# A substitution with its operands turned round, its place in the order of a scan's steps, and the order of the projections beside it

## The chip, the cores and the metric

The kernel runs on one core of a Trainium2 chip. The metric is the time of one execution on the device, in microseconds (us). Five engines work beside each other, each through its own queue in a fixed order: TensorE (PE, matrix products, with its weight loads as PEld), VectorE (DVE), ScalarE (ACT), GpSimd (POOL) and SyncE (SP, which issues most of the DMAs). An engine that comes to an instruction whose input isn't there waits, and all behind it in its queue waits too.

## The reference

Two layers. In each, a normalised and modulated input `h` (768 tokens: 256 of context, 512 latent) is multiplied by one large matrix `w_in`; its columns feed three mixers, their gates and the merge:

```python
h = rms_norm(x, norm_g) * (1.0 + scale) + shift
za, ga, zb, gb, zc, gc, zg = jnp.split(h @ w_in, list(IN_CUTS), axis=-1)
ya = rwkv7_branch(za, ...)            # two scans over time, forward and backward
yb = dense_block_attention(...)       # from zb
yc = window_attention(...)            # from zc
m = sum(sigmoid(zg_n) * ((y_n * silu(g_n)) @ w_branch_out[n]))
x_new = x + gate * (m @ w_out)
```

The scan of the first mixer is the step `S <- S diag(w) - (S kk)(kk*a)^T + v k^T`, `y = S r`, for each of eight heads and two directions. The first layer gives an output for context and latent tokens, the second for the latent ones alone.

## The kernel before, in words

The scan is done in 12 chunks of 64 tokens (`NCH`), the eight heads and two directions beside each other. Within a chunk the recurrence is a triangular system, so each chunk needs the inverse of a triangular 64x64 matrix. `rwkv_inverse` (L654) makes them for four chunks at a time (`NS` = 4), in three groups (`NG`): for each 64x64 matrix it inverts the two 32x32 blocks on the diagonal by substitution on DVE and makes the third block from them with small matmuls (`zp`, L691, and `yp`, L699).

The substitution (L673 to L678) runs over `j` from 30 down to 1. For each `j` there are two DVE instructions over `j * (31 - j)` elements of each of 128 partitions: a product of a broadcast column and a broadcast row into `tmp` (L676), and its addition to `YK` (L678). `YK` is a view of `YB`, whose rows of 64 elements lie behind each other, so that in the view `Y3` (`p i j`) the last index steps over 64 elements, 256 bytes. Ahead of it stands a transposition on DVE (L666), behind it two more (L681, L682). The function is a generator. Its first part, up to the `yield` at `j` = 22, holds the loads of `TT` and the first nine pairs, the second goes to `j` = 12, the third to the transpositions; three more hold the small matmuls.

`rwkv` (L510) runs the scan. First comes group 0's inverse, then `FILL[l][1]` steps of other work to cover it, and then the twelve steps of the scan, `rwkv_step` (L705). Each step is cut in three: `Rp` from the state, `Up` with the inverse, `Sp` and `Yp` to the new state and the output; in between stand copies on ACT and DVE (L714, L727, L728) and the state's update on DVE (L738, L739). Between them stand parts of `scores` for the chunk after next (matmul `scps`, then L642 and L644 on DVE), of `readout` (L564) and of the fill. After each of the first three steps of a group one part of the next group's inverse is emitted (L557), in the fourth step the parts with matmuls (L552).

The fill is the rest of `h @ w_in`: `tiles` (L1454) is a generator over tiles of 128 columns, and `pace(n)` (L1468) takes `n` steps of it. A tile over both segments is 48 matmuls in 8 steps (the narrow tile `T_KR` has 5). Beside them, twice in a tile, `side` gives a piece of the modulation `ada` (matmul `modps`, then L261 and L269 or L272 on DVE). `proj` (L764) ends a tile: a "raw" tile is one copy on ACT for each segment; a "silu" tile is an ACT instruction (L777) and a DVE instruction (L779) for each, and only behind it is the PSUM bank free for the next tile. The tiles `g` have two banks (`GB`); a tile over both segments takes both. Each half tile needs a weight block that ACT splits (L165) and POOL subtracts (L166). The tiles of the last gate (`T_ZG`, "tanh") come last, and what the scan leaves of them stands between the matmuls of the later stages and then by itself (`gates`, L1496).

The order of the work: the scheduler puts each instruction into its engine's queue at build time, by a priority and by when it expects its inputs. `band(b)` sets the priority: `SERVE` comes first, then `B + 1` (the scan), `B + 3` (attention), `B + 4` (fill). Within a band the order of the program counts. `in_line()` (L148) keeps all TensorE instructions of the scan in the order of the program; the other engines' instructions are free to change places. The small matmuls `zp` of a group thus hold up everything behind them on TensorE until the substitution is done.

Of the kernel before, what the change touches and what calls it, by code (L numbers as in the profile page):

```python
# [14 lines left out]
ALU = mybir.AluOpType  # L15
# [4 lines left out]
P = 128  # L20
# [9 lines left out]
GB, RB, CB = 2, 3, 2  # L30


FILL = ((48, 36, 2, (2, 2, 2), (3, 3, 3), 2), (72, 56, 4, (2, 2, 2), (3, 3, 3), 2))

QUEUES = (("scalar", "sync", "sync", "scalar"), ("sync", "scalar", "sync", "sync"))

# [1 line left out]
NS, NG = 4, 3  # L38
# [22 lines left out]
def build(tc, A, out):  # L61
# [13 lines left out]
    @contextmanager  # L75
    def band(b):

        keep, mine = tc.cur_priority, bands.get(b, b * 1000000)
        tc.cur_priority = mine
        yield  # L80
        bands[b] = tc.cur_priority
        tc.cur_priority = keep
# [427 lines left out]
    def rwkv(l, D, last, DL, B, pace, zlast):  # L510

        with tc.tile_pool(name="rw", bufs=1, reuse_waits="tile") as rp:
            yo = rp.tile([P, 4, T], F32, name="yo")
            st = {"seen": set(), "S": None}
            parts, YB = {}, {}

            def scores(i):
                if i < NCH:
                    parts[i] = yield from rwkv_scores(l, last, rp, i)

            def invert(g):
                if g < NG:
                    YB[g] = rp.tile([P, 32, 64], F32, tag="YB", name="YB", bufs=2)
                    yield from rwkv_inverse(l, rp, g, YB[g])

            def rest(*gens):
                for g in gens:
                    for _ in g:
                        pass

            with band(B + 1):
                rest(scores(0), scores(1))
                ahead = invert(0)
                for _ in range(3):
                    next(ahead)
            with band(B + 4), tc.issue_after(zlast):
                pace(FILL[l][1])
            with band(B + 1), in_line():
                for _ in ahead:
                    pace(FILL[l][2])  # L540
                ahead = out = iter(())
                for i in range(NCH):
                    if i % NS == 0:
                        rest(ahead)
                        ahead = invert(i // NS + 1)
                    nxt = scores(i + 2)
                    step = rwkv_step(l, last, i, yo, st, DL, rp, parts.pop(i), YB[i // NS])
                    for n in FILL[l][3 if i % NS < NS - 1 else 4]:
                        next(step, None)
                        next(nxt, None)  # L550
                        if i % NS == NS - 1:
                            next(ahead, None)  # L552
                        next(out, None)
                        pace(n)
                    rest(step, nxt)
                    if i % NS < NS - 1:
                        next(ahead, None)  # L557
                    if i in READY and (i > 3 or not last):
                        rest(out)
                        out = readout(l, D, rp, yo, READY[i])  # L560
                for _ in out:
                    pace(FILL[l][5])

# [90 lines left out]
    def rwkv_inverse(l, rp, g, YB):  # L654
# [3 lines left out]
        for b0 in (0, 64):  # L658

            DMA.dma_start(TT[b0:b0 + 32], tt_d[l][b0:b0 + 32, :, cs])  # L660
            DMA.dma_start(TT[b0 + 32:b0 + 64, :, :, 0:32], tt_d[l][b0 + 32:b0 + 64, :, cs, 32:64])
        inv = rp.tile([P, 1536], F32, tag="inv", name="inv")
        MB, tmp = inv[:, 0:1024], inv[:, 1024:1536]
        YK = YB[:, :, 32:64]
        TT4 = TT.rearrange("p c s t -> p (c s) t")
        V.transpose(MB, TT4[:, :, 0:32].rearrange("p n j -> p j n"))  # L666

        M3 = MB.rearrange("p (j i) -> p i j", i=32)
        Y3 = YK.rearrange("p j i -> p i j")
        G.affine_select(YK, MB.rearrange("p (j i) -> p j i", i=32),  # L670
                        [[1, 32], [-1, 32]], ALU.is_gt, 0.0, base=0, channel_multiplier=0)
        V.memset(YB.rearrange("p n c -> p (n c)")[:, 32:2048:65], 1.0)
        for j in range(30, 0, -1):  # L673
            n = 31 - j
            t3 = tmp[:, 256 * (j % 2):256 * (j % 2) + j * n].rearrange("p (i c) -> p i c", c=n)
            V.tensor_tensor(t3, M3[:, 0:j, j:j + 1].to_broadcast([P, j, n]),  # L676
                            Y3[:, j:j + 1, j + 1:32].to_broadcast([P, j, n]), ALU.mult)
            V.tensor_tensor(Y3[:, 0:j, j + 1:32], Y3[:, 0:j, j + 1:32], t3, ALU.add)  # L678
            if j in (22, 12):
                yield  # L680
        V.transpose(YB[:, :, 0:32].rearrange("p n j -> p j n"), YK)  # L681
# [753 lines left out]
    for l in range(2):  # L1435
# [18 lines left out]
        def tiles():  # L1454

            zb = [(T_CQ + j, zb_d[l][j], (LAT,) if last and j < 2 else BOTH, "raw") for j in range(4)]
            zc = [(T_ZC + j, zb_d[l][4 + j], (LAT,) if last and j < 4 else BOTH, "raw") for j in range(6)]
            ga, gb, gc = ([(t + j, g_d[l][4 * n + j], segs, "silu") for j in range(4)]
                          for n, t in enumerate((T_GA, T_GB, T_GC)))
            todo = zb[2:] + zc[4:] + zc[:4] + zb[:2] + ga + gb if last else zb + ga + gb + zc  # L1460
            todo += gc + [(T_ZG + j, th_zg[l][j], segs, "tanh") for j in range(24)]
            for a in todo:
                yield from proj(l, hh, hl, *a, side)
                yield
# [193 lines left out]
```

## Time and profile before

| | |
|---|---|
| median of 3 runs | 2422.4 us (2420.09 to 2424.84) |
| the profiled execution's own time | 2427.43 us |
| its span in the trace | 2425.7 us |
| mean granted TensorE clock | 0.948 of full speed |
| TensorE busy | 2148.9 us (89%) |
| VectorE busy | 1271.8 us (52%) |
| substitution, L676 and L678, 360 instructions | 183.7 us of VectorE |

The profile is one execution. The busy share of an engine is a mean over stages, so what bounds a stage is read from that stage: how long TensorE was busy in it, and what ended its waits. The granted clock is given as a share of 2.4 GHz; the other level is 1.2 GHz. The first layer's scan, with its first inverse, lies at 360 to 640 us from the span's start, the second layer's at 1660 to 1940 us.

### The profile page before, as it was taken

The numbers are of one execution on the slowest core, as the hardware profiler recorded it, in microseconds if no ns is written. First come the engines' busy times: TensorE is split into PE (matmuls) and PEld (weight loads), VectorE is DVE, ScalarE is ACT, GpSimd is POOL, SyncE is SP. The second block draws the span as 40 slices with busy tenths as digits, with TensorE's granted clock in tenths as the row PEclk, the third lists the DMA queues.
The fourth block names the chain that finished last, engine by engine and source line by source line (L and its number), as shares of the span: only waits on it lengthen the run. The fifth ranks groups of instructions, "written<-read, shape, count | busy, mean of one in ns | idle before, by whom it ended". The sixth has DMA issues, their size and how long they took to land. (4 is left out here: it accounts for less than half of the span.)

```text
span 2425.7 us, 42832 instructions
## 1 busy us (share of the span) xinstructions
PE 2148.9 (89%) x16824; PEld 1647.0 (68%) x16824; DVE 1271.8 (52%) x2300; ACT 891.7 (37%) x1654; POOL 870.0 (36%) x699
## 2 busy tenths in 40 slices
PE   7986896887998999899888998799868998999989
PEld 4765674766887667766767786567656876666667
DVE  4475326865338664366135256725668457554423
ACT  3443211233354333543213345332323455434322
POOL 1255211111123344444334224553211144454564
PEclk9988998998999999999989999899978999999999
DMA  7155665555251012511686414566444262102385
GB/s 249 60 144 175 194 197 138 138 132 136 74 170 50 31 44 84 189 33 51 205 256 188 134 57 123 163 206 169 121 113 101 86 209 92 48 18 70 106 261 168
DMA packets 330442, 314.25 MB, mean 130 GB/s; under 512 B 112768, under 2 KB 239488, under 8 KB 330240
## 3 DMA queue, kind: packets, MB, share of 16 engines
q1 hardware_dynamic: 312432, 281.87, 39.5%
q10 hardware_dynamic: 17808, 29.63, 3.9%
q8 instruction: 133, 2.18, 0.4%
q14 instruction: 69, 0.57, 0.1%
HBM read 213.64 MB, written 97.78 MB: 128 GB/s over the span
## 5 line engine op out<-in xcount | busy, mean ns | idle before, releaser
L166 POOL TENSOR_TENSOR wl<-wf,wh 128x512 fp32r<-128x512 f32 x316 | 425.7, 1349 | 1064.0 <-ACT wh L165 977.2
L154 PE MATMUL g<-hh,wh 128*128 128x512 f32 (+1 forms) x1264 | 471.3, 373 | 19.2 <-DVE st L779 10.2
L154 PE MATMUL g<-hh,wl 128*128 128x512 f32 (+1 forms) x1264 | 457.0, 362 | 1.5 <-POOL wl L166 1.4
L154 PE MATMUL g<-hl,wh 128*128 128x512 f32 (+1 forms) x1264 | 456.4, 361 | 0.0
L165 ACT CAST wh<-wf 128x512 fp32r<-128x512 f32 x316 | 195.1, 619 | 500.7 <-PE g L154 249.3
L154 PEld LDWEIGHTS g<-hh,wh 128*128 128x128 f32 x1264 | 249.1, 197 | 71.9 <-issue 15.4
L154 PEld LDWEIGHTS g<-hh,wl 128*128 128x128 f32 x1264 | 249.3, 197 | 41.1 <-issue 7.9
L154 PEld LDWEIGHTS g<-hl,wh 128*128 128x128 f32 x1264 | 249.9, 198 | 40.1 <-issue 11.4
L886 POOL TENSOR_TENSOR acc<-acc,pe 128x512 f32<-128x512 f32 (+2 forms) x128 | 146.2, 1142 | 141.2 <-ACT pe L882 131.7
L882 ACT ACTIVATE pe<-stp 128x256 f32<-128x256 f32 (+2 forms) x224 | 114.4, 522 | 201.1 <-PE stp L154 194.4
L864 DVE TENSOR_REDUCE mx<-mps 128x1 f32<-128x384 f32 (+2 forms) x256 | 127.8, 535 | 69.2 <-PE mps L154 67.0
L154 PE MATMUL yps<-pe,vh 128*64 128x256 f32 (+1 forms) x704 | 133.3, 389 | 0.0
L678 DVE TENSOR_TENSOR YB<-YB,inv 128x30 f32<-128x30 f32 (+9 forms) x180 | 96.4, 536 | 5.3
L154 PE MATMUL g<-yh,wh 128*128 128x512 f32 (+1 forms) x224 | 81.4, 368 | 19.9 <-DVE zt L1368 11.4
L1368 DVE SCALAR_TENSOR_TENSOR zt<-zt,g 128x512 f32<-128x512 f32 (+1 forms) x56 | 31.7, 576 | 117.6 <-PE g L154 85.3
L676 DVE TENSOR_TENSOR inv<-inv,YB 128x30 f32<-128x30 f32 (+9 forms) x180 | 87.3, 485 | 8.5 <-issue 2.3
L777 ACT ACTIVATE st<-g 128x256 f32<-128x256 f32 (+1 forms) x108 | 56.6, 524 | 89.1 <-PE g L154 83.7
L154 PE MATMUL g<-yl,wh 128*128 128x512 f32 (+1 forms) x224 | 83.5, 374 | 6.1 <-POOL yl L1353 6.1
L154 PE MATMUL gc<-hh,wh 128*128 128x512 f32 x192 | 76.7, 400 | 8.6 <-ACT hh L325 4.5
L154 PE MATMUL g<-yh,wl 128*128 128x512 f32 (+1 forms) x224 | 80.4, 363 | 0.0
L154 PE MATMUL scps<-AR,BK 64*128 64x128 f32 (+1 forms) x768 | 65.5, 296 | 14.5 <-DVE TR L644 10.6
L154 PE MATMUL gc<-hl,wh 128*128 128x512 f32 x192 | 78.0, 406 | 0.1
(395 smaller groups left out, 4358.2 us busy)
## 6 DMA issues: line engine op xcount, KB each, us to landing
wf<-w_in SPq DMA_DIRECT2D x163, 256.0 KB, 3.1
wf<-ada_w SPq DMA_DIRECT2D x84, 256.0 KB, 4.0
wf<-w_in ACTq DMA_DIRECT2D x77, 256.0 KB, 3.0
bkd<-bk SPq DMA_DIRECT2D x16, 768.0 KB, 6.3
zt<-thzg SPq DMA_DIRECT2D x48, 256.0 KB, 3.8
wf<-w_bo SPq DMA_DIRECT2D x40, 256.0 KB, 3.5
thzg<-st SPq DMA_DIRECT2D x24, 384.0 KB, 2.4
md<-zt SPq DMA_DIRECT2D x32, 256.0 KB, 3.5
```

The costliest lines, as they stand in the source:

```text
L154: queued(TE.matmul(o, l, r, start=start, stop=stop, **kw))
L165: S.copy(wh, w32)
L166: eng.tensor_tensor(wl, w32, wh.bitcast(F32), ALU.subtract)
L676: V.tensor_tensor(t3, M3[:, 0:j, j:j + 1].to_broadcast([P, j, n]), Y3[:, j:j + 1, j + 1:32].to_broadcast([P, j, n]), ALU.mult)
L678: V.tensor_tensor(Y3[:, 0:j, j + 1:32], Y3[:, 0:j, j + 1:32], t3, ALU.add)
L777: S.activation(t[:, sl], p, AF.Tanh, scale=0.5)
L864: V.tensor_reduce(mx, ps, AX.X, ALU.max)
L882: S.activation(e, st, AF.Exp, scale=scale)
L886: G.tensor_tensor(acc, keep.pop(0, acc), e, ALU.add)
L1368: V.scalar_tensor_tensor(th, th, 1.0, p_, ALU.add, ALU.mult)
```

## The change

Four edits, in three functions and one table.

- The substitution holds the same numbers in the same places, but its two instructions run with the index of neighbouring elements innermost: `YK` itself is the operand instead of its turned view, and `M3` is viewed as `p j i`.
- The first part of `rwkv_inverse`, up to a new `yield`, now holds the loads of `TT` alone.
- In the scan, the next group's loads are emitted at the head of the group's first step, and right behind them all three parts of its substitution, in the band `B + 2`, which was not used before and comes after `B + 1`. Nothing is emitted after the first three steps any more.
- In the first layer `FILL[0][1]` is 48 instead of 36, and its projections run in the order `zb`, `zc`, `ga`, `gb` (raw ones first) instead of `zb`, `ga`, `gb`, `zc`. The second layer's table and order are as they were.

```diff
-FILL = ((48, 36, 2, (2, 2, 2), (3, 3, 3), 2), (72, 56, 4, (2, 2, 2), (3, 3, 3), 2))
+FILL = ((48, 48, 2, (2, 2, 2), (3, 3, 3), 2), (72, 56, 4, (2, 2, 2), (3, 3, 3), 2))
...
                 ahead = invert(0)
-                for _ in range(3):
+                for _ in range(4):
                     next(ahead)
...
                     if i % NS == 0:
                         rest(ahead)
+
                         ahead = invert(i // NS + 1)
+                        next(ahead, None)
+                        with band(B + 2):
+                            for _ in range(3):
+                                next(ahead, None)
...
                     rest(step, nxt)
-                    if i % NS < NS - 1:
-                        next(ahead, None)
...
             DMA.dma_start(TT[b0 + 32:b0 + 64, :, :, 0:32], tt_d[l][b0 + 32:b0 + 64, :, cs, 32:64])
+        yield
...
-        M3 = MB.rearrange("p (j i) -> p i j", i=32)
-        Y3 = YK.rearrange("p j i -> p i j")
+        M3 = MB.rearrange("p (j i) -> p j i", i=32)
...
-            t3 = tmp[:, 256 * (j % 2):256 * (j % 2) + j * n].rearrange("p (i c) -> p i c", c=n)
-            V.tensor_tensor(t3, M3[:, 0:j, j:j + 1].to_broadcast([P, j, n]),
-                            Y3[:, j:j + 1, j + 1:32].to_broadcast([P, j, n]), ALU.mult)
-            V.tensor_tensor(Y3[:, 0:j, j + 1:32], Y3[:, 0:j, j + 1:32], t3, ALU.add)
+            t3 = tmp[:, 256 * (j % 2):256 * (j % 2) + j * n].rearrange("p (c i) -> p c i", c=n)
+            V.tensor_tensor(t3, M3[:, j:j + 1, 0:j].to_broadcast([P, n, j]),
+                            YK[:, j + 1:32, j:j + 1].to_broadcast([P, n, j]), ALU.mult)
+            V.tensor_tensor(YK[:, j + 1:32, 0:j], YK[:, j + 1:32, 0:j], t3, ALU.add)
...
-            todo = zb[2:] + zc[4:] + zc[:4] + zb[:2] + ga + gb if last else zb + ga + gb + zc
+            todo = (zb[2:] + zc[4:] + zc[:4] + zb[:2] if last else zb + zc) + ga + gb
```

## Rows read from the trace of the kernel before

**Rows 1.** The page's part 1: busy time, share of the span, instructions of each engine.

```profile
PE 2148.9 (89%) x16824; PEld 1647.0 (68%) x16824; DVE 1271.8 (52%) x2300; ACT 891.7 (37%) x1654; POOL 870.0 (36%) x699
```

**Rows 2.** Busy time by stretch of both scans; "582.00" is a stretch without substitution.

```profile
core 0: us, PE busy (x) PEld busy (x) DVE busy (x) ACT busy (x) POOL busy (x), PEclk, DMA share, GB/s
360.00:425.00 65.00, 41.34 (x479) 31.43 (x479) 40.08 (x79) 12.07 (x20) 11.40 (x10) 0.82 0.56 143
425.00:500.00 75.00, 64.00 (x990) 52.48 (x984) 56.66 (x120) 19.59 (x38) 9.79 (x8) 0.93 0.52 138
500.00:582.00 82.00, 62.82 (x878) 51.06 (x879) 59.51 (x121) 26.86 (x47) 12.14 (x10) 0.85 0.51 135
582.00:640.00 58.00, 57.67 (x1071) 50.12 (x1071) 21.39 (x47) 20.16 (x38) 7.68 (x6) 1.00 0.38 100
1660.00:1722.00 62.00, 47.09 (x233) 36.89 (x232) 44.41 (x70) 15.41 (x25) 21.86 (x18) 0.86 0.50 138
1722.00:1808.00 86.00, 64.94 (x1124) 52.87 (x1122) 57.87 (x115) 26.68 (x48) 14.34 (x11) 0.84 0.49 117
1808.00:1888.00 80.00, 69.45 (x1215) 57.10 (x1215) 58.59 (x116) 25.28 (x48) 13.37 (x11) 0.89 0.46 111
```

**Rows 3.** Waits of TensorE, 373 to 425 us: total us, times, longest us.

```profile
PE zp L154 <- DVE inv L682: 23.3, 1, 23.3
```

**Rows 4.** Waits of TensorE, 425 to 582 us.

```profile
PE modps L154 <- DVE mod L272: 5.3, 3, 2.9
PE modps L154 <- DVE mod L269: 4.3, 2, 4.1
PE Rp L154 <- DVE UV L714: 4.0, 1, 4.0
PE scps L154 <- DMA AR<-ard: 3.9, 1, 3.9
```

**Rows 5.** Waits of TensorE, 1680 to 1722 us.

```profile
PE g L154 <- DVE st L779: 9.8, 3, 4.8
PE zp L154 <- issue: 5.1, 1, 5.1
```

**Rows 6.** Waits of TensorE, 1722 to 1890 us.

```profile
PE zp L154 <- DVE inv L682: 14.8, 2, 12.7
PE scps L154 <- DVE TR L644: 9.3, 3, 3.8
```

**Rows 7.** DVE in order of time, first inverse: start us, us, engine, line, operation.

```profile
376.96 0.15 DVE L676 TENSOR_TENSOR inv<-inv,YB 128x30 f32<-128x30 f32 x1 [0.35 <-DVE st L779]
...
389.14 1.53 DVE L676 TENSOR_TENSOR inv<-inv,YB 128x228 f32<-128x228 f32 x1
...
395.07 0.56 DVE L676 TENSOR_TENSOR inv<-inv,YB 128x240 f32<-128x240 f32 x1
395.67 0.58 DVE L678 TENSOR_TENSOR YB<-YB,inv 128x240 f32<-128x240 f32 x1
...
409.13 0.21 DVE L676 TENSOR_TENSOR inv<-inv,YB 128x30 f32<-128x30 f32 x1
409.38 0.21 DVE L678 TENSOR_TENSOR YB<-YB,inv 128x30 f32<-128x30 f32 x1
```

**Rows 8.** DVE groups by shape, 360 to 1900 us: busy us, mean ns, idle before.

```profile
L1159 DVE TENSOR_TENSOR rp<-gqm,scq 128x256 f32<-128x256 f32 x8 | 3.0, 415 | 0.0
...
L1159 DVE TENSOR_TENSOR rp<-gqm,sck 128x64 f32<-128x64 f32 x8 | 1.4, 215 | 0.0
```

**Rows 9.** PE in order of time, around the first inverse's end.

```profile
389.11 0.39 PE L154 MATMUL g<-hl,wh 128*128 128x512 f32 x1
412.85 1.92 PE L154 MATMUL zp<-inv,TT 32*32 32x32 f32 x64 [23.35 <-DVE inv L682]
...
415.29 0.63 PE L154 MATMUL g<-hh,wh 128*128 128x512 f32 x1
```

**Rows 10.** Busy time in the last stretch of the first layer's gate tiles.

```profile
1160.00:1181.30 21.30, 20.65 (x118) 17.84 (x117) 1.87 (x3) 5.61 (x12) 6.55 (x6) 1.00 0.61 185
```

**Rows 11.** POOL's weight subtraction, 376 to 410 us: ns min/median/max.

```profile
L166 POOL TENSOR_TENSOR wl<-wf,wh x3: 1270/1279/1448, 378.6 to 389.0; 128x512 fp32r<-128x512 f32 x3
```

## The prediction

> **What bounds the kernel now.** I read the page's busy times first, then the stretches of both scans, then what ended TensorE's waits there, and last the instructions behind the longest wait. TensorE is busy for 89% of the span and no other engine for more than 68% [rows 1], so a gain has to come from TensorE's idle time. The stretches say where it is [rows 2]: length less busy time gives 23.7, 11.0 and 19.2 us in the first layer (360 to 582) and 14.9, 21.1 and 10.6 us in the second (1660 to 1888), 100 us in all. The stretch from 582 to 640, the same steps with no substitution beside them, has 0.3. So the idle time comes with the substitution.
>
> The clock adds to it. The six stretches show mean clocks of 0.82 to 0.93 [rows 2], the one without substitution 1.00. With two levels, 1.00 and 0.50, the low one held for 2 x (1 - clock) x length: 23, 11, 25, 17, 28 and 18 us, 122 in all. Part of that is the idle time itself; in the rest TensorE worked at half speed, as behind the wait of the first inverse, where a matmul of 512 columns took 0.63 instead of 0.39 us [rows 9]. At least 122 - 100 = 22 us of work ran so, at most all 122. I take 55, since a spell of low clock lasts on behind each wait, and half of that, 27 us, is lost. With everything ideal the scans could give 100 + 27 = 127 us.
>
> What the waits are: in the first layer one of 23.3 us for the end of the inverse [rows 3], then many small ones for DVE instructions queued between those of the substitution, L269 and L272 of `ada` with 9.6 us and the state's copy L714 with 4.0; one of 3.9 us is a DMA's and not DVE's [rows 4]. In the second layer `zp` and the silu tiles' L779 in the first inverse [rows 5], and `zp` with 14.8 us and L644 with 9.3 in the two groups after it [rows 6].
>
> **The change, part by part.** I sum against the profiled execution, 2427.4 us (span 2425.7 and 1.7 around it), which lies 5.0 us above the median of the three runs.
>
> *Operands turned.* In one inverse the first product, whose 30 elements are neighbours, took 0.15 us; the last, whose 30 elements step over 256 bytes, 0.21. From 30 to 240 stepping elements the product goes from 0.21 to 0.56 us, 1.67 ns an element, the addition from 0.21 to 0.58, 1.76 ns [rows 7]. No substitution of neighbouring elements beyond 30 is in the trace. The nearest rows are another DVE product with neighbours innermost, 0.215 us for 64 elements and 0.415 for 256, 1.04 ns an element [rows 8]. The saving is 0.63 + 0.72 = 1.35 ns an element; the pairs of one inverse have the sum of j x (31 - j) = 4960 elements. Each run of j neighbours still starts with a step, and there are 465 runs. So 4495 x 1.35 ns = 6.1 us for each inverse, of about 30. Bounds: nothing, if the step isn't what costs, and 4960 x 1.35 = 6.7; I take 6.1, for the two small rows of the same line point the same way. It counts only where the inverse's end, or an instruction queued behind it, is waited for.
>
> *First inverse, first layer, with 12 more steps of fill.* A step is 6 matmuls; 118 took 20.65 us [rows 10], so 12 steps are 12.6 us, and the three pieces of `ada` that come with them are 8 matmuls each, some 2 us. They leave the stretch of gate tiles that ends at 1181, which was 97% busy and had no wait [rows 10], so what is moved is saved there in full; if it had only filled holes, the move would be worth nothing there. The fill ended at 389.5 and will end at 404.1. The inverse ended at 412.8 [rows 9]: 6.1 us earlier by the operands, 0.7 by fewer silu instructions between. Against this stands POOL. One product took 1.53 us where its neighbours take 0.56 [rows 7], as POOL's weight subtraction of 1.27 us ran beside it [rows 11]; three more half tiles are now subtracted within the inverse, +3.0 us. It ends at 409.0, and the idle time goes from 23.6 to 4.9 us: -18.7. Bounds: -12.6 with no gain from the operands, -23 with all idle time gone. The Trainium skill, "SBUF — State Buffer", Who interferes with whom, says that a DVE instruction with two SBUF inputs and a GpSimd instruction that reads SBUF lock each other out, the loser for the other's whole length. By it a faster substitution doesn't shorten these collisions; the 1.53 us agrees, and without it the term would be 3 us larger.
>
> *First inverse, second layer.* Fill and order are unchanged. The idle time, 14.9 us [rows 2], is split between the silu tiles' waits and `zp` [rows 5]; its sum is the inverse's end less TensorE's own work, so it falls by the 6.1 us and no more.
>
> *Groups 1 and 2: order.* The substitution comes behind all of the scan's own instructions in priority, so `ada`'s additions, the state's copies and L642/L644 no longer queue behind a run of it. A single instruction of 0.2 to 0.45 us can still stand ahead, as the queue is fixed at build time. The new loads in front are two pairs of DMAs on SP ahead of the step's `BK`, `AR` and weight loads; they hold SP up only while `TT` is still read by `zp`, as before. Nothing waits for them but L666, which can start some us sooner.
>
> *Groups 1 and 2: more silu tiles.* In the first layer, steps 100 to 154 of the fill fall into these groups. By the new order they are 6.75 tiles, all silu; before (88 to 142) they were 0.6 silu and the rest raw. Each silu tile has two DVE instructions, 0.42 and 0.68 us by the slope of [rows 8], so DVE gets 6.8 us more, 3.4 for each group, and a TensorE wait for L779 where these come late.
>
> By group. First layer, group 1 (11.0 us idle): DVE gets 6.1 less and 3.4 more, and the `ada` wait of 4.1 goes; -6. Group 2 (19.2): substitution has room there, since `zp` of this group isn't among the waits; `ada` and the state's copies go, the DMA's 3.9 and some of the readout's stay: -8. Second layer, group 1 (21.1): TensorE waits for the end of the substitution, 12.7 us at once [rows 6], so DVE is the bound; 6.1 from the operands and 2 from the earlier start, -8. What is late next is still `zp`. Group 2 (10.6): L644's waits turn into a shorter one for `zp`: -5. The bounds are 0 and all of each.
>
> *Clock.* Where waits fall by half, I give back that share of the low-clock loss: 2 + 1 in the first inverses, 3, 3, 4 and 4 in the groups, 17 of 27 us.
>
> **Sum**: 18.7 + 6.1 + 6 + 8 + 8 + 5 = 52 us of idle time and 17 of clock: 69. 2427.4 - 69 = 2358, less the 5 by which the profiled run lies above the median: 2353 us.
>
> **Rivals.**
>
> *Demotion only moves the waits.* If the substitution, now last in line, ends as late as before, the groups' small waits turn into one long wait at `zp`, with a lower clock behind it. For: DVE bounds the second layer's group 1. Against: the first layer's `zp` isn't late. The first inverses give 25 + 3; the groups only 10 instead of 27, and 5 of clock: 43 us, 2379.
>
> *The step over 256 bytes isn't the cost.* Then 12.6 us from the fill, some 15 from order, 8 of clock: 36, 2386. Against: the slopes of [rows 7] and [rows 8].
>
> *All DVE waits vanish.* The scans become like the stretch from 582 to 640: 127 us less some 10 of the DMA's and readout's waits: 2427.4 - 117 - 5 = 2305.
>
> *Slower: silu tiles behind the substitution.* A first-layer tile takes both banks of `g`, so TensorE can't begin the next before L779 has freed them. If each of the 13 or 14 L779 of groups 1 and 2 waits as long as the longest in the second layer, 4.8 us [rows 5], that is 65 us idle and 15 of clock against the 69 gained: 2353 + 80 = 2433. It decides from about 4 us a wait. For: those three waits happened. Against: L779 is in the band that comes first, and then at most one substitution instruction stands ahead of it.
>
> *No effect*, since the scheduler already placed what matters: 2418 to 2427. Against it stands the moved fill alone.
>
> **How the numbers follow.** Forecast 0.52 (2330 to 2372), demotion 0.17, operands 0.10, all gone 0.13, no effect 0.04, slower 0.04. A measurement of this kernel can tell some 0.2% (4.8 us) from no change. Faster 0.92, same 0.04, slower 0.04. The range takes in the two weaker cases and reaches half way to the ideal: 2316 to 2394.
>
> **What would show it.** Substitution of 240 elements: 0.41 to 0.44 us where no POOL subtraction runs, and some 147 us for all 360 instead of 184. `zp` waits in the first layer's first inverse: about 5 us instead of 23. Waits for L269 and L272 in the scan: under 2 us. Second layer, group 1: a `zp` wait of 5 to 12 us still there. Clock of the six stretches: 0.93 or more. I am wrong if the 240-element time stays above 0.5, if waits for L779 in 425 to 582 exceed 10 us, or if the gate stretch of the first layer doesn't end earlier than the scan does by some 12 us.

## The result and the profile after

| | before | after | ratio, 95% interval |
|---|---|---|---|
| beside each other | 2423.6 us (4 runs) | 2396.2 us (4 runs, 2389.3 to 2402.6) | 0.988 (0.985 to 0.992) |
| again, later | 2423.8 us (17 runs) | 2393.9 us (5 runs, 2388.0 to 2400.4) | 0.987 (0.985 to 0.990) |
| the profiled execution: span | 2425.7 us | 2387.3 us | |

The change is faster, by 27 us where 70 were forecast, and 2396 us lies above the range's upper end of 2394. The page's part 1 of after, to be held against [rows 1]:

```profile
PE 2147.1 (90%) x16824; PEld 1645.6 (69%) x16824; DVE 1223.6 (51%) x2300; ACT 891.4 (37%) x1654; POOL 868.6 (36%) x699
```

TensorE's idle time (span less busy) went from 276.8 to 240.2 us, its busy time only from 2148.9 to 2147.1. So of the two parts of the sum the idle time gave 36.6 of 52 us, and the clock, which shows in the busy time, next to nothing of 17. Where the idle time went, by the stretches that answer to [rows 2] (columns as there; the second layer's stretches are taken 40 us earlier, as the scan's end there came 38 us earlier), with the stretch from 640 to 800 beside them: the end of the first layer's scan, whose last matmul ends at 673.9 us before and 665.9 after, and the first part of its attention. From 640 us to there TensorE is idle for 0.3 us at most.

```profile
360.00:425.00 65.00, 58.76 (x560) 45.26 (x558) 35.52 (x83) 15.53 (x27) 17.66 (x14) 0.97 0.61 181
425.00:500.00 75.00, 61.62 (x914) 50.24 (x908) 49.14 (x116) 19.17 (x35) 9.76 (x9) 0.89 0.59 142
500.00:582.00 82.00, 70.20 (x1141) 58.66 (x1139) 56.70 (x137) 30.20 (x54) 13.55 (x11) 0.92 0.53 141
640.00:800.00 160.00, 144.18 (x959) 120.19 (x957) 85.84 (x180) 75.64 (x144) 42.30 (x31) 0.95 0.28 95
1620.00:1682.00 62.00, 58.86 (x303) 47.63 (x302) 29.77 (x57) 17.48 (x31) 23.91 (x19) 0.94 0.69 182
1682.00:1768.00 86.00, 64.35 (x1015) 52.14 (x1015) 55.80 (x127) 27.46 (x47) 18.00 (x15) 0.82 0.52 123
1768.00:1850.00 82.00, 75.18 (x1427) 61.63 (x1423) 56.63 (x127) 29.72 (x57) 13.40 (x11) 0.94 0.51 125
```

The first inverse has 6.2 us of idle time left (23.7 before), group 2 of the first layer 11.8 (19.2). But group 1 (425 to 500) has 13.4 where it had 11.0, and 640 to 800 has 15.8. Before, that stretch had 10.6:

```profile
640.00:800.00 160.00, 149.36 (x1121) 127.15 (x1120) 88.76 (x184) 77.92 (x149) 43.08 (x32) 0.98 0.31 100
```

Some of TensorE's waits after, from 425 to 500, from 500 to 582, and from 640 to 800 (total us, times, longest us):

```profile
PE modps L154 <- DVE mod L272: 6.3, 2, 6.1
PE scps L154 <- DMA AR<-ard: 6.1, 2, 3.1
...
PE scps L154 <- DMA AR<-ard: 7.3, 1, 7.3
...
PE krp L154 <- DMA krr<-zbd: 4.5, 1, 4.5
PE pr L154 <- DVE yo L761: 2.2, 1, 2.2
```

Against [rows 4]: the `ada` wait that should go is there with one of 6.1 us, and the wait for `AR`, a load, grew from 3.9 to 13.4 us in the two groups. `krp` waits 4.5 us for a load too (1.7 before).

The substitution did what was said of it. In the first inverse (columns as in [rows 7]), with POOL's weight subtraction in the last line:

```profile
394.34 0.41 DVE L679 TENSOR_TENSOR inv<-inv,YB 128x240 f32<-128x240 f32 x1
394.78 0.41 DVE L681 TENSOR_TENSOR YB<-YB,inv 128x240 f32<-128x240 f32 x1
395.22 1.37 DVE L679 TENSOR_TENSOR inv<-inv,YB 128x240 f32<-128x240 f32 x1
394.96 1.37 POOL L166 TENSOR_TENSOR wl<-wf,wh 128x512 fp32r<-128x512 f32 x1 [6.90 <-ACT wh L165]
```

A product or addition of 240 elements takes 0.41 us instead of 0.56 to 0.58. The third line shows a collision: it ends 0.26 us after POOL's subtraction. All 360 instructions take 140.2 us instead of 183.7.

### The profile page after: what moved, and what is told of

It is laid out like the page before. It is cut to its first block, busy times and chain, and to the rows that moved or that the text cites. A ratio compares the mean times of both kernels' runs of the same rounds, so it can differ in the third digit from the quotient of the medians.

```text
span 2387.3 us, 42836 instructions
## 1 busy us (share of the span) xinstructions
PE 2147.1 (90%) x16824; PEld 1645.6 (69%) x16824; DVE 1223.6 (51%) x2300; ACT 891.4 (37%) x1654; POOL 868.6 (36%) x699
## 5 line engine op out<-in xcount | busy, mean ns | idle before, releaser
L645 DVE TENSOR_TENSOR AR<-scps,cst 64x256 f32<-64x256 f32 x96 | 40.1, 418 | 89.1 <-PE scps L154 87.9
L154 PE MATMUL scps<-AR,BK 64*128 64x128 f32 (+1 forms) x768 | 64.1, 293 | 17.0 <-DMA AR<-ard 13.4
L889 POOL TENSOR_TENSOR acc<-pe 128x512 f32<-128x512 f32 (+1 forms) x48 | 52.6, 1097 | 69.6 <-ACT pe L885 68.6
```

The source lines that it names most:

```text
L154: queued(TE.matmul(o, l, r, start=start, stop=stop, **kw))
L645: V.tensor_tensor(AR[oth, pds, 2 * par, :], ps[oth, :, a0:a0 + 64], msk("ms", oth), ALU.mult)
L889: G.tensor_tensor(acc, keep.pop(0, acc), e, ALU.add)
```

## The experiments

The change has separable parts, so I first ran them alone and left them out singly, and then followed the waits that appeared. Each ratio is to the kernel before on the same chip. The column "low" is TensorE's busy time that lies in stretches granted 1.2 GHz, worked out by laying the trace's clock over TensorE's busy intervals. Busy time less half of it is 2059 to 2066 us in all 20 traces, so what the busy time differs by from kernel to kernel is the clock's, but for at most 7 us.

| kernel | ratio, 95% interval | idle, whole span | low | idle 640 to 800 |
|---|---|---|---|---|
| before | 1 | 276.8 | 171 | 10.6 |
| after (two profiles) | 0.988, 0.987 | 240.2, 243.8 | 164, 177 | 15.8, 16.8 |
| e1 operands alone | 0.983 (0.982 to 0.985) | 247.9 | 157 | 10.4 |
| e2 order alone | 1.001 (0.999 to 1.002) | 278.1 | 182 | 10.8 |
| e4 steps and raw first alone | 1.005 (1.004 to 1.007) | 277.2 | 189 | 16.1 |
| e6 after, without order | 0.990 (0.988 to 0.992) | 249.3 | 168 | 16.5 |
| e7 after, without raw first | 0.987 (0.985 to 0.989) | 240.6 | 185 | 16.2 |
| e8 after, without 48 steps | 0.986 (0.984 to 0.988) | 247.8 | 163 | 10.8 |
| e9 operands and order | 0.982 (0.980 to 0.984) | 246.9 | 150 | 10.1 |
| g1 operands, 12 steps more at the scan's end | 0.984 (0.982 to 0.987) | 245.7 | 154 | 13.5 |
| f1 after, chunk loads first | 0.999 (0.997 to 1.000) | 273.0 | 177 | 15.9 |
| f4 after, fill's loads on ACT's queue | 0.984 (0.981 to 0.986) | 245.6 | 153 | 16.4 |
| f5 operands, fill's loads on ACT's queue | 0.979 (0.977 to 0.981) | 232.9 | 161 | 10.3 |
| h1 operands, order, fill's loads on ACT's queue | 0.979 (0.976 to 0.981) | 229.0 | 161 | 10.5 |
| h2 h1, readout's store on POOL's queue | 0.979 (0.977 to 0.982) | 234.8 | 156 | 9.8 |
| h3 h2 with 48 steps | 0.985 (0.983 to 0.988) | 250.0 | 171 | 16.3 |
| h1 with 24 steps | 0.986 (0.983 to 0.988) | 251.4 | 163 | 17.4 |
| h1 with 30 steps | 0.987 (0.984 to 0.989) | 249.2 | 163 | 14.4 |
| b1 before, fill's loads on ACT's queue | 0.993 (0.991 to 0.996) | 258.0 | 189 | 10.6 |

**The parts alone.** e1 has the turned operands only:

```diff
-        M3 = MB.rearrange("p (j i) -> p i j", i=32)
-        Y3 = YK.rearrange("p j i -> p i j")
+        M3 = MB.rearrange("p (j i) -> p j i", i=32)
...
+            t3 = tmp[:, 256 * (j % 2):256 * (j % 2) + j * n].rearrange("p (c i) -> p c i", c=n)
+            V.tensor_tensor(t3, M3[:, j:j + 1, 0:j].to_broadcast([P, n, j]),
...
```

> The kernel before with the operands of the substitution turned and nothing else. My theory: the gain of the change was given back in the first layer by late loads and by the queue order behind them, not by the operands. Then the operands alone give their 6 us in each first inverse (idle time of TensorE in 360 to 425 about 17.5 instead of 23.7 us, in the second layer's first inverse about 9 instead of 14.9), 4 to 6 in each of the groups in which DVE is late, no new wait for AR in 425 to 500: about 20 us faster, 2400 us. Rival, the operands matter only in the first inverses: 12 us, 2410. Rival, the faster substitution itself upsets the groups: under 6 us, 2417 or more.

41 us faster (2388.6 against 2429.2), twice the theory's 20 and more than the whole change. Idle time fell by 28.9 us and the low-clock busy time by 15, and no wait for `AR` appeared in 425 to 500. So the other parts together take back some 10 us: by the ratios after is 10 to 12 us slower than e1.

e2 has the early loads and the band `B + 2` only, at the old operands, steps and order of projections:

```diff
+                        next(ahead, None)
+                        with band(B + 2):
+                            for _ in range(3):
+                                next(ahead, None)
...
```

> The kernel before with the next group's loads early and its substitution in the band behind the steps; operands, fill and order of the projections as before. Theory (late loads come from the moved fill): the first inverse keeps its 23 us of idle time, in which SP loads the next chunks, so in 425 to 500 there is no wait for AR above 1 us, the waits for L269 and L272 in both groups fall from 9.6 to under 3 us, and the time falls by 10 to 20 us: 2403 to 2413. Rival, the early loads of TT alone hold up SP: waits for AR of 5 us or more in 425 to 500 here as well, and the idle time there stays at 11 us or more. Rival, the demotion only moves the waits: zp waits of 5 us or more in the first layer's groups, within 5 us of before.

No difference, and no wait for `AR` in 425 to 500. The `ada` waits did not fall: in 425 to 582 they are 14.0 us against 9.6. Nor did they turn into a wait for `zp`, which has 0.2 us there. TensorE's waits, 425 to 500, kernel e2:

```profile
PE modps L154 <- DVE mod L269: 5.0, 2, 4.8
PE modps L154 <- DVE mod L272: 4.1, 1, 4.1
```

One such wait can be followed on DVE in order of time in e9, which has the same order with the turned operands. `modpt`, which L272 reads, began on TensorE at 471.49 with four small matmuls; L272 ran at 476.08:

```profile
469.81 0.21 DVE L681 TENSOR_TENSOR YB<-YB,inv 128x30 f32<-128x30 f32 x1
470.06 1.97 DVE L684 STREAM_TRANSPOSE YB<-YB 128x1024 f32<-128x1024 f32 x1
471.88 0.66 DVE L741 TENSOR_TENSOR So<-So,Sp 128x512 f32<-128x512 f32 x1
472.47 1.21 DVE L685 STREAM_TRANSPOSE inv<-YB 128x1024 f32<-128x1024 f32 x1
473.60 0.65 DVE L742 TENSOR_TENSOR So<-So,DL 128x512 f32<-128x512 f32 x1
474.18 0.74 DVE L761 TENSOR_TENSOR yo<-yo,Yp 128x256 f32<-128x256 f32 x2
474.95 1.10 DVE L717 COPY UV<-So 64x512 f32<-64x512 f32 x1
476.08 0.16 DVE L272 TENSOR_TENSOR mod<-modpt,pp 128x4 f32<-128x4 f32 x1
```

Ahead of it stands not a single instruction of 0.2 to 0.45 us but a transposition of 1.2, among the state's update, `yo` and the state's copy, all in an order fixed at build time. L741, L742, L761 and L717 are the scan's own and don't belong to the band that was lowered. That the other waits came about in the same way is not shown.

e4 has the 48 steps and raw projections first, with the old operands and order:

```diff
-FILL = ((48, 36, 2, (2, 2, 2), (3, 3, 3), 2),
+FILL = ((48, 48, 2, (2, 2, 2), (3, 3, 3), 2),
...
-            todo = zb[2:] + zc[4:] + zc[:4] + zb[:2] + ga + gb if last else zb + ga + gb + zc
+            todo = (zb[2:] + zc[4:] + zc[:4] + zb[:2] if last else zb + zc) + ga + gb
```

> The kernel before with 48 steps of fill over the first inverse instead of 36 and raw projections first; operands and order as before. The 12.6 us of moved work leave the end of the gates, and the first inverse's idle time goes from 23.7 to about 11. Theory (the moved fill takes the time in which SP loaded the next chunks): waits for AR of 4 us or more in 425 to 500, and so only 6 to 10 us faster: 2413 to 2417. Rival (the moved fill costs nothing): no new wait for AR, 12 us or more: 2411 or less. Rival (the raw projections first, so silu tiles in the groups, cost): waits for the silu tiles' second instruction of 5 us or more in 425 to 582.

13 us slower, worse than any of the expectations. TensorE's waits in 425 to 500, and two of those in 582 to 800, kernel e4:

```profile
PE modps L154 <- DVE mod L272: 7.6, 2, 7.4
PE scps L154 <- DMA AR<-ard: 7.1, 2, 3.9
...
PE scps L154 <- DMA AR<-ard: 9.6, 1, 9.6
...
PE krp L154 <- DMA krr<-zbd: 4.8, 1, 4.8
```

These are the waits of after, with nothing else of the change in the kernel. So the fill brings them. The idle time of the whole span is the same as before (277.2 against 276.8 us): the 15.1 us that went ahead of `zp` came back in the waits behind it. What makes the kernel slower is busy time, 11.4 us more in the profile, of which the low clock accounts for 9 ("low" 189 against 171).

Left out singly, they give the same picture; e6 takes the order out of after (the diff of e2 undone), e7 the raw projections first, e8 the 12 steps:

```diff
-            todo = (zb[2:] + zc[4:] + zc[:4] + zb[:2] if last else zb + zc) + ga + gb
+            todo = zb[2:] + zc[4:] + zc[:4] + zb[:2] + ga + gb if last else zb + ga + gb + zc
...
-FILL = ((48, 48, 2, (2, 2, 2), (3, 3, 3), 2),
+FILL = ((48, 36, 2, (2, 2, 2), (3, 3, 3), 2),
```

> The changed kernel with loads and substitution in the old places and the old band; turned operands, 48 steps and raw projections first stay. Theory (moved fill together with early loads of TT make AR late): the waits for AR in 425 to 500 shrink from 6.1 to under 3 us; the L269 and L272 waits come back to 5 to 10 us; time within 5 us of the changed kernel, 2391 to 2401. Rival, the new order costs by itself: 5 to 15 us faster than the changed kernel. Rival, the new order is what brings the gain: 10 to 20 us slower than the changed kernel, 2406 to 2416.

e6 has 0.990: leaving the order out costs some 5 us, no more than the runs of one kernel differ, and the `AR` waits of 6.1 us in 425 to 500 stay, so the early `TT` loads aren't their cause.

> The changed kernel itself once more, so that it and the kernels beside it share one chip. By the first times it is 1.2% faster than before (0.985 to 0.992), the turned operands alone were 1.7%. Theory: part of the change gives back 10 us or more of what the operands bring, so its ratio stays above 0.986. Rival: the two are equal and the first times were from an unlucky chip: 0.983 to 0.986.

> The changed kernel with the first layer's projections in the old order (gates ga, gb ahead of the raw zc); operands, loads and band, 48 steps stay. Theory (the 48 steps cost, through the loads that they bring forward): as the changed kernel within 5 us, waits for AR of 5 us or more in 425 to 500 stay. Rival (raw projections first is what costs): 8 to 15 us faster than the changed kernel, near the operands alone with 2388.

> The changed kernel with 36 steps of fill over the first inverse instead of 48; operands, loads and band, raw projections first stay. Theory (the 48 steps cost): zp waits 12 to 17 us again in the first inverse, but no wait for AR above 2 us in 425 to 500, and 5 to 12 us faster than the changed kernel. Rival (raw first costs): the AR waits stay, and it is 5 to 12 us slower than the changed kernel.

After is 0.987 here too, e7 and e8 0.987 and 0.986: leaving out one half of the fill change doesn't bring e1's time, so each half by itself costs nearly what both cost. With 36 steps (e8) the `AR` waits in 425 to 500 and the extra idle time in 640 to 800 go, and `zp` waits 16.5 us again; with 48 and the old order of projections (e7) they stay, 7.2 us. By the theory e8 should have been 5 to 12 us faster than after, and it was 3. Why raw first costs something without the 48 steps isn't settled; its trace has 8.1 us of `AR` wait in 500 to 582.

> Turned operands, early loads and the band behind the steps; 36 steps and the old order of the projections. The ledger so far, as ratios to before: operands 0.983, order 1.001, steps and raw first 1.005, all together 0.987 to 0.988. Theory (the parts add up, the order is worth nothing): 0.983 to 0.986, idle time of TensorE in 640 to 800 about 10.5 us as before. Rival (the order costs once the substitution is faster): 0.987 or more. Rival (it brings something then, as leaving it out of the changed kernel cost 0.3%): 0.981 or less.

e9 takes 2383.8 us, 0.982: with the substitution short the order may be worth 3 us, within the intervals. This is the change without its fill part, and by the ratios it is some 13 us below after. (e9 is e1 with the diff of e2.)

**Where the 12 steps are missed.** g1 leaves the first inverse alone and takes 12 steps more in the last four chunks of the scan:

```diff
                     for n in FILL[l][3 if i % NS < NS - 1 else 4]:
+                        n += i >= NCH - NS and not last
```

> The operands alone (36 steps, old order), but each of the last four chunks of the first layer's scan takes 3 more steps of fill, 12 in all; the first inverse is as it was. The question is where 12 steps are missing when an earlier place takes them. Theory (they are the cover of the attention's first part, not of the pure gate stretch at the end): the wait of krp for krr goes from 1.4 to 4 us or more in 640 to 800 and the idle time there from 10.4 to about 16, the whole is no faster than the operands alone and may be 5 us slower. Rival (they leave the end of the gates, where nothing waits): idle time in 640 to 800 stays at 10 to 11 us. In 425 to 582 nothing should differ from the operands alone.

The wait of `krp` came, with no edit ahead of the scan's last four chunks. Of TensorE's waits in 640 to 800, in e1:

```profile
PE krp L154 <- DMA krr<-zbd: 1.4, 1, 1.4
```

and in g1:

```profile
PE krp L154 <- DMA krr<-zbd: 4.8, 1, 4.8
```

The idle time in 640 to 800 rose to 13.5, not to 16; the time of the whole kernel is within the intervals of e1's. The load that `krp` waits for lands 35 to 37 us after the scan's last matmul in e1, g1 and after alike. TensorE's matmuls of fill (`g`) from there to `krp`, their busy time and, in brackets, their number, in e1 (as in before), g1 and after:

```profile
659.50:695.10 35.60, 32.39 (x173) 26.37 (x173) 1.10 (x2) 3.33 (x7) 1.00 0.62 190
669.10:705.50 36.40, 29.70 (x161) 24.40 (x161) 0.00 (x0) 3.31 (x7) 1.00 0.55 169
665.90:703.20 37.30, 28.60 (x152) 23.25 (x152) 0.00 (x0) 3.31 (x7) 0.97 0.52 163
```

So of the 72 matmuls that the 12 steps are, 12 in g1 and 21 in after had been part of the cover of the attention's first stage, and are missing there.

**Why AR is late.** SP's queue in order of time, the loads of chunk 3 (columns: start, us, queue, line, operation), kernel before:

```profile
395.97 0.63 SPq L615 DMA_DIRECT2D AR<-ard  x1
396.64 2.37 SPq L617 DMA_DIRECT2D AR<-ard  x2
```

and after:

```profile
436.27 0.37 SPq L246 DMA_DIRECT2D wf<-ada_w  x1
436.69 0.57 SPq L664 DMA_DIRECT2D TT<-ttd  x1
437.30 0.68 SPq L616 DMA_DIRECT2D BK<-bkd  x1
440.24 0.35 SPq L162 DMA_DIRECT2D wf<-w_in  x1
440.63 0.65 SPq L246 DMA_DIRECT2D wf<-ada_w  x1
441.32 0.60 SPq L618 DMA_DIRECT2D AR<-ard  x1
```

Before, they were issued in the 23 us in which TensorE stood still. After, the fill runs there, and the loads are issued 45 us later. The fill's weight loads take turns with the scan's loads, and those that wait for a buffer hold the queue: SP's own waits, 421 to 447 us of after, in their first two rows:

```profile
SPq L246 <- POOL wl L166: 6.9, 3, 2.5
SPq L162 <- PE modps L154: 5.5, 2, 3.3
```

f1 emits the loads of chunks 2 and 3 ahead of the first inverse:

```diff
                 rest(scores(0), scores(1))
+                early = {n: scores(n) for n in (2, 3) if not last}
+                for n in early:
+                    next(early[n])
                 ahead = invert(0)
...
```

> The changed kernel with the loads of chunks 2 and 3 (BK, AR, UV) of the first layer emitted ahead of the first inverse and its fill; nothing else differs. Theory (chunk 3's AR stands behind the fill's weights and TT on SP's queue): the waits for AR in 425 to 500 go from 6.1 to under 1 us and the L272 wait of 6.1 there with them, 8 to 15 us faster than the changed kernel: about 2380 to 2388. Rival (the late AR is only a sign; DVE is as late anyway): AR waits go, zp or DVE waits of the same length come, within 4 us of the changed kernel. Rival (the early loads hold up the fill's own weights): waits for wh or wl over 4 us in 360 to 425, no gain.

The `AR` waits of group 1 went, as the theory has it. The one of group 2, whose chunks' loads were left where they were, did not: with 7.2 us it comes at 594.9, behind the stretch to 582, as the scan runs 29 us later. The kernel lost 27 us against after: the loads of chunks 2 and 3 now stood on SP ahead of `TT` of the first inverse itself, which began at 416 instead of 378.5 us, and `zp` waited 36.2 us. So the loads were badly placed, and that pointed to what I had not asked: what holds up `TT`?

f4 (on after) and f5 (on e1) put the fill's weights on ACT's queue:

```diff
-QUEUES = (("scalar", "sync", "sync", "scalar"),
+QUEUES = (("scalar", "scalar", "sync", "scalar"),
```

> The changed kernel with the first layer's fill weights (w_in and ada_w, from the first inverse to the scan's end) loaded on ACT's queue instead of SP's, as the second layer does it. Theory (AR comes late because the loads of the scan stand on SP between the fill's weight loads, which wait for their buffers): the waits of scps for AR in 425 to 582 go from 13.4 to under 3 us, the L272 wait of 6 goes too if it came from late TT, and the time falls by 8 to 18 us against the changed kernel: 0.980 to 0.984. Rival (the bandwidth or the buffers make AR late, not the queue): the waits stay at 10 us or more. Rival (ACT now stands before its issues, waiting for buffers): waits for ACT's UV, yo, Rs grow by 10 us or more and eat it.

> The turned operands alone with the same move of the first layer's fill weights to ACT's queue. Theory: the AR wait of 3.8 us in 500 to 582 goes, 3 to 8 us faster than the operands alone, 0.980 to 0.982. Rival (ACT held up by its issues): slower than the operands alone by 5 us or more.

f4: the `AR` wait in 425 to 500 is gone, the one in 500 to 582 stays with 7.1 us, L272 stays with 6.3; 0.984. Half of the theory holds. f5 takes 2377.0 us, 10 us below e1 by the ratios, and it brought what wasn't expected: no wait for `zp` at all in the first inverse, with 36 steps of fill. The first transposition of the first inverse (L666, L670 with the order part) starts like this in before:

```profile
373.56 1.99 DVE L666 STREAM_TRANSPOSE inv<-TT 128x1024 f32<-128x1024 f32 x1
```

and in h1, which has the same new queue:

```profile
343.59 2.01 DVE L670 STREAM_TRANSPOSE inv<-TT 128x1024 f32<-128x1024 f32 x1
```

That is 30 us earlier. In before the four loads of `TT` leave SP from 344 to 367.5 us, with weight loads and stores of finished tiles between them, and the last lands at 371.1. In h1 the last lands at 333.9. The transposition follows 2.5 and 9.7 us behind it: there it stands in DVE's queue behind instructions of the fill and of `ada`. b1 makes this one move in the kernel before, with the slow substitution:

> The kernel before with nothing but the first layer's fill weights on ACT's queue: old operands, old order, 36 steps. Theory (the loads of TT, held up on SP, set when the first inverse ends): its first transposition starts at about 344 us instead of 373.6, the zp wait of 23.3 us in 360 to 425 goes to under 3 us although the substitution is as long as before, and the kernel is 8 to 14 us faster: 0.994 to 0.997. Rival (the length of the substitution sets it): zp still waits 15 us or more, no difference. Rival (the waits of the groups, which the slow substitution keeps, take it back): the zp wait goes, ratio 0.998 to 1.002.

b1 has 0.993, 16 us faster. The transposition starts at 343.58, the last one ends at 389.5, and `zp` waits for nothing until TensorE comes to it at 407.5. All of TensorE's waits from 360 to 425, kernel b1:

```profile
PE modpt L154 <- DVE row L261: 4.8, 2, 3.3
PE g L154 <- DVE st L779: 1.0, 1, 1.0
PE g L154 <- POOL wl L166: 0.4, 1, 0.4
PE modps L154 <- DVE mod L269: 0.3, 1, 0.3
```

So with `TT` in time the wait of 23.3 us in [rows 3] isn't there, even with the slow substitution: the late loads on SP made it, and the length of the substitution came on top. The idle time of the whole span fell by 18.8 us with the old substitution in all six inverses.

**Does the fill pay when the queues are clear?** h1 is e9 with the new queue; h2 moves the readout's store (L606) to POOL's queue; h3 is h2 with 48 steps:

```diff
-            DMA.dma_start(cols(yg_d[l][p]), y)
+            G.dma_start(cols(yg_d[l][p]), y)
...
-FILL = ((48, 36, 2, (2, 2, 2), (3, 3, 3), 2),
+FILL = ((48, 48, 2, (2, 2, 2), (3, 3, 3), 2),
```

> Turned operands, early loads and the band behind the steps, and the first layer's fill weights on ACT's queue; 36 steps, old order of the projections. Theory (the parts add up): 0.979 for operands with the queue, 0.1 to 0.2% more from the order: 0.976 to 0.979. Rival (the order is worth nothing once the loads are clear of SP): 0.979 to 0.981.

> As h1_order_queue, but the readout's store (L606) is issued from POOL's queue instead of SP's. Theory (the store waits on SP for DVE's instructions and holds up the AR loads behind it): the wait of scps for AR or for the store in 500 to 582 goes to under 1 us, 2 to 6 us faster than h1_order_queue. Rival (DVE is late there anyway): the AR wait goes and a DVE wait of the same length comes, no difference. Rival (POOL now stands before the store, and its weight subtractions come late): waits for wl of 3 us or more in both scans, slower.

> As h2_store_pool, but with 48 steps of fill over the first inverse. Theory (with both queues clear only the lost cover is left): no AR wait in 425 to 582, but 4 us or more for krp in 640 to 800 and more time there at the low clock, so within 4 us of h2_store_pool. Rival (the AR waits were all of it): 5 to 12 us faster than h2_store_pool.

h1 takes 2375.6 us and is the fastest kernel here, level with f5, some 20 below after. In h2 the `AR` wait in 500 to 582 is 1.3 us against 1.8: the new queue had shortened it already, and the time is the same. h3 lost 16 us. The matmuls `zp` of the first inverse (ns min/median/max, first and last start), h2:

```profile
L154 PE MATMUL zp<-inv,TT x128: 190/191/212, 404.2 to 410.2; 32*32 32x32 f32 x128
```

and h3:

```profile
L154 PE MATMUL zp<-inv,TT x128: 190/191/212, 423.9 to 430.5; 32*32 32x32 f32 x128
```

TensorE doesn't wait for `zp` in either, so the steps have no long wait to fill and set the scan back by 20 us. Nothing of it comes back later: the first matmul of the gate output (`yh`) is 21 us later as well. From the scan's end to there TensorE has 72 matmuls less, but 10 us more of idle time (35.3 against 25.6), and the matmuls of fill from the scan's end to `krp` are 153 instead of 174.

Was fill over the inverse worth less than nothing, then, and would fewer steps be better? The last two kernels are h1 with 24 and with 30 in place of 36:

> As h1_order_queue with 24 steps of fill over the first inverse instead of 36. There the inverse ends at 386.7 us and zp begins at 402.8, so 16 us of fill stand before zp without need. Theory (the steps are worth more as cover of the attention's first part): zp begins at 388 to 392 with a wait under 4 us, the first layer's gates end 8 to 14 us earlier than in h1_order_queue, 0.971 to 0.975. Rival (as the prediction had it: moved steps are a plain gain): slower than h1_order_queue by the 12.6 us that are moved back, 0.983 or more. Rival (no matter where): 0.977 to 0.980.

> As h4_steps_24 with 30 steps. Theory: between the two, zp at about 396, no wait for it, 0.974 to 0.977. Rival (moved steps are a plain gain): 6 us slower than h1_order_queue, 0.981. Rival (no matter where): 0.977 to 0.980.

No: they have 0.986 and 0.987, 17 and 19 us slower than h1 by the ratios. With 24 `zp` begins at 388.0, 15 us earlier, but the scan's three groups have 11 us more idle time and the stretch from there to `yh` 7 more. From the scan's end to `krp` they have 153 and 164 matmuls of fill, against 173 in h1, although the steps were moved to behind the scan: the call of `pace` that stands right behind it, and does nothing with 36 or 48 steps, here takes 11 and 5. So taking steps away in front thins that place as adding them does, and my theory falls in this form. What stands: of the four numbers 36 is best, 6 or 12 fewer and 12 more cost 16 to 19 us, and moved steps aren't a plain gain in either direction. Why the order leaves fewer matmuls there, and why 24 loses in the scan's groups, stays open.

## Why the prediction was wrong

By the profiles three terms make up most of what is missing from the sum: the clock gave 3.5 of 17 us, group 1 of the first layer lost 2.4 where 6 were to come, and the stretch from 640 to 800, which the sum doesn't have, lost 5.2. The other idle terms came within 2.3 us each of what was told, two of them by luck.

**Operands: right.** The forecast was 0.41 to 0.44 us and some 147 for all 360; 0.41 and 140.2 came. The rival that the step over 256 bytes isn't the cost is out. Alone they brought 41 us; in the profiles these are 28.9 of idle time and 10 of busy time. That is more than the whole change gained.

**First inverse, first layer: near in idle time, wrong in worth.** Idle time there fell by 17.4 us where 18.7 were told. But the step "They leave the stretch of gate tiles that ends at 1181 ... so what is moved is saved there in full" failed. Between the scan's end and `yh` TensorE had 12.0 us less of work at 2.4 GHz, as told, but the stretch got only 5.9 us shorter, and 3.1 in the second profile: idle time there rose by 3.3 and 5.0, what is lost by the low clock by 2.8 and 3.9. Of the 72 matmuls 21 had not stood in the dense stretch at the end but ahead of `krp`, where 640 to 800 has 5.2 us more of idle time. I had named the case in which the move is worth nothing, and read only the place where the queue of fill ends, not the places between that live on it. `yh` came 14 us earlier in after (1170.1 against 1184.0), and in e1, without the move, 15 (1168.8).

It also missed what sets the inverse's end. It ended at 415.0, not 409.0: it began 5.0 us later (378.54 against 373.56), 3.3 of these because the last load of `TT` landed later still (374.4 against 371.1). The fill ended 8.7 us later than told too, at 412.8 instead of 404.1, so that the idle time came out near is luck. The prediction never asked why L666 began when it did, and its "So the idle time comes with the substitution" is answered by b1, where the longest wait is gone and the substitution is the old one. POOL's collisions were seen rightly: six instructions of the substitution took 1.25 to 1.37 us beside POOL's weight subtractions of 1.29 to 1.45. The Trainium skill, "SBUF — State Buffer", Who interferes with whom, calls the pair of ports that the two engines share an exclusive lock, and says that the order of issue, not the shape, decides who blocks. The trace agrees: a product that takes 0.41 us alone took 1.37 beside a subtraction that had begun 0.26 us before it.

**The loads: wrong.** "Nothing waits for them but L666" looked at the loads that the change moves. The ones that mattered were those the fill brings along: 12 more steps bring weight loads of `w_in` and `ada_w` on SP, in front of chunk 3's `AR`. That made 6.1 us of wait in group 1, which had 2.4 us more of idle time instead of 6 less. With these loads on ACT's queue (f4) that wait is gone. What made the one in group 2 grow from 3.9 to 7.3 us stays open: in f4 it is there with 7.1.

**Order: wrong.** It was to bring a good part of the 14 us of the first layer's groups; alone it brought nothing (1.001). In the one wait that was followed, what stands ahead of L272 are instructions of 0.65 to 1.2 us, most of them the scan's own, which the lowered band leaves where they are. That group 2 came out near, with 7.4 of 8 us, is luck: the operands alone give 6.0 there (e1), and the prediction had given it to the order.

**Clock: mis-sized, and the largest miss.** 17 us were to come back. Low-clock busy time fell from 171 to 164 us, worth 3.5; in the second profile of after it rose to 177. In e1 and e9 it fell by 15 and 22, worth 7 and 11. My 55 us of low clock on work in the six stretches were too few: by the same overlay it is 74. In after it is 56 there, so 9 us came back, and 640 to 800 took 3 of these (12.1 against 6.5 us at the low level). The step that failed is "Where waits fall by half, I give back that share of the low-clock loss". Where idle time didn't fall (425 to 500, and 1682 to 1768, which now has the 6.4 us of `zp` too) low-clock work rose by 2 us each, and outside the six stretches, where the sum has nothing, it rose by 11. In before much of the low clock lay on the long wait, where it cost nothing: of 23.9 us in 360 to 425 only 4.6 fell on work. In e4 and b1, where that wait goes and the substitution is the old one, low-clock work of the whole span rose by 18 and 17 us.

**The second layer** came out near the forecast: idle time fell by 5.4 us in its first inverse (with the 6.4 us of `zp` that now lie behind 1682), and by 5.8 and 3.7 in the groups, where 6.1, 8 and 5 were told.

**The rest is the profiled run.** After's lies 6.9 us below the median of its four runs, and before's lay above its own: the traces differ by 38 us and the medians by 27.

**The rivals.** Silu tiles behind the substitution didn't happen: the silu instruction ended no wait of TensorE in 425 to 582 of after. That the demotion would turn the small waits into one at `zp` didn't happen in the first layer's groups either: in e2 the small waits stayed where they were.

## What to carry to other kernels

Work that fills a wait is taken from somewhere: look for every stage that has the same work between its own waits, not only for the place where its queue ends, and try both directions, for here fewer steps in front left less cover behind the scan as well. Before the length of a late chain is shortened, ask why its first instruction starts when it does; here loads of the fill stood on the same queue, waited for their buffers and held up the loads of the critical chain, and one word in a table of queues removed a wait of 23 us that a faster substitution and more fill had been built against. What a change to an order fixed at build time is worth, only a run of it alone shows: the three parts here were worth 41 us, nothing and minus 13.

## What was not expected of the hardware

TensorE's time at 2.4 GHz, busy time less half of what lies in 1.2 GHz stretches, is constant to 0.3% (2059 to 2066 us) over 20 traces of 19 kernels: but for these 7 us, all that an order changes is idle time and where the low clock falls. The runs of one kernel differ by 13 us in four runs of after (2389.3 to 2402.6), by 9 in four of before and by 14 in 17, so that one profile against another can be 11 us off the medians.
